# Values of the next key group fetched and split four steps later in a one-core attention block

## The chip, the cores and the metric

The kernel runs on one core of one Trainium2 chip. The metric is the device time of one execution in microseconds (us), taken as the median of several runs. The core has five engines that matter here: TensorE (PE in the profile, with its weight loads shown apart as PEld), VectorE (DVE), ScalarE (ACT), GpSimd (POOL) and SyncE (SP), which issues most of the loads.

## The reference, cut to what matters

The block is one layer of a hybrid generator over 512 latent tokens of width 2048, with 256 context tokens, all in float32. Attention has 12 query heads of width 128 in 4 key groups, three heads to a group. The keys and values of a group are 512 latent and 256 context rows, 768 in all:

```
q = _rope(_rmsnorm(heads(h @ w_q)), cos, sin) * q_scale
k = concat(_rope(_rmsnorm(heads(h @ w_k))), _rmsnorm(heads(hc @ w_k)))
v = concat(heads(h @ w_v), heads(hc @ w_v))
attn = softmax(q @ k.T) @ v
y_a = (attn * silu(z_a)) @ w_pa
y_b = (fourier_mix(u_b) * silu(z_b)) @ w_pb
out = rmsnorm(x + gate * ((g_a * y_a + g_b * y_b) @ w_o))
```

## The kernel before, in words

**Numbers in two halves.** Every float32 product is made of three matmuls on split numbers: `split_from` (L177) has ACT write a rounded high part (L178) and DVE the remainder, the low part (L179); `mm3` (L332) then multiplies high by high, high by low and low by high (L334 to L336). So every weight, key and value that comes from memory is loaded into a raw buffer, split by ACT and DVE, and only then used by PE.

**Stages.** The projections come first (eight groups of weight products, written in `Group.steps`, L1041), and leave queries, keys, values and gates in DRAM (`qz_d`, `k_d`, `v_d`, `g_d`). Attention follows, from about 815 us to 1015 us of the profile: a loop of `NSTEP` = 48 steps (L1639), one for each quarter (128 query rows) of each of the 12 heads, and three steps more that let the last ones end. Then come branch A's projection, the merge and the output projection.

**A step of attention.** Step `i` computes 128 x 768 scores (`scores`, L1475): DVE takes the row maximum (L1486), ACT the exponential (L1488). `turn` (L1500) transposes the exponentials of step `i - 1` on PE (L1504) and splits them (tiles `pth`, `ptl`). `values` (L1511), called at every even step from 4 on, multiplies two steps' worth of them with the group's values: `values(m)` runs at step `2m + 4`, and its matmuls write `banks` and read `pth`, `ptl` (a row `banks<-pth,s`). Its transposes of the gate path have the line L1519. A key group serves 12 score steps, and since `values` comes four steps after the first of its scores, group n's keys are first used at step 12n and its values at step 12n + 4.

**Work between the steps.** `filler` (L1432) computes branch B's projection as 64 small parts spread over the steps, by `fill`. It has four chunks; each needs two pieces of weights (`("pab", j, pc)`), and fetches them with its first part: chunks 1, 2 and 3 at steps 11, 23 and 36. The modulation's gate rows (`use_gate`, L1321, DVE line L1324) are used at the 16 steps of `GATE_STEPS`.

**The list of loads.** `stream` (L196) puts every piece that is to be loaded on one list, `todo`, in the order in which it will be asked for. `start_load` (L199) takes the list's head, gives it a raw buffer of those that are free, and has SP issue the DMA (L214); `load_more` (L225) does that as long as a raw buffer is free and fewer than eight pieces are ahead. In attention there are seven raw buffers: four of the pool `wp`, `raw1`, and two that are given back at step 33. `get` (L293) hands out the piece that is next on the list. It first splits that piece, and those of the next two that are loaded already, but a piece of values (`"V"`) only when it is itself asked for; a piece of keys or a gate row is handed out raw. Taking a piece out frees its raw buffer for the list's head.

**Keys and values.** `stream_keys` (L406) lists the keys of a group and right behind them its values. `get_keys` (L1340), called at steps 10, 22 and 34 for groups 1, 2 and 3, transposes the keys on PE (L1344), splits them into two tiles of `tiles` (L372), and gets the values, which are split into two more. These tiles are slots of a free list (`take`, L322: the slot that has been free for the longest goes first; `give` puts one at the end), which also serves the exponentials, the queries and branch A's operands. `values` gives a group's four slots back after its last use.

**Who sets the order.** The code's order is a priority only. The framework's planner lays down each engine's order of instructions before the run; it lets an instruction go ahead of earlier code when by its own estimate the inputs are there and the tile's slot has been let go. At run time every engine takes its instructions in that order and waits on semaphores.

Of the kernel before, what the change touches and what calls it, by code (L numbers as in the profile page):

```python
# [120 lines left out]
def block_kernel(ctx, tc, xT, ctx_rows, ctx_toks, x, c_row, w_ss, w_gate, vecs, qkg, rope, dft_c, dft_s,  # L121
# [74 lines left out]
    def stream(key, src, *a, **k):  # L196
        todo.append(Piece(key, src if isinstance(src, list) else [src], *a, **k))
# [174 lines left out]
    def tiles(key):  # L372

        new = [take((1024,), F32R) for _ in range(2)]
        kept.setdefault(key, []).extend(new)
        return new
# [28 lines left out]

    def stream_keys(g):  # L406
        stream(("K", g), flat(k_d[g]), NKEY, KT, "raw")
        stream(("V", g), flat(v_d[g]), NKEY, KT, dst=lambda: tiles(g))

    which_ctx = [0]  # L410
# [6 lines left out]
    for g in range(LAST + 1):  # L417
        for name in ONE_GROUP:
            if (g, name) == (LAST, "Q4"):
                stream_keys(0)  # L420
            if g == KV:
                f = CTX_FORMS.index(next(f for n, f, _, _ in PRODUCTS if n == name))
                stream(("cf", name), cf_d[:, :, f].rearrange("i p j c -> p i j c"), 1024, 8, dst=ctx_tiles)
            stream_product(name, g, w_g[g], BY_DVE_GATES)
            for pc in range(4):
                p = context_piece(g, name, pc)
                if p:
                    src, cols = (ctx_toks[p[1]], 1024) if p[0] == "cn" else (ctx_rows[p[1]], 4 * C)
                    stream(p, src, cols, 1, "raw")
                    todo.insert(len(todo) - 4 + pc, todo.pop())  # L430
            for pc in range(4):
                if (g, name, pc) in GATE_AT:
                    q = GATE_AT[g, name, pc]
                    stream(("gate", q), w_gate[q], 1024, 1, "raw")
                    e = todo.pop()
                    at = next(i for i, x in enumerate(todo) if x.key == (name, g, pc))
                    todo.insert(at + 1, e)
# [3 lines left out]
    for n, j in enumerate(CHUNKS):  # L441
        for pc in BRANCH_B:
            stream(("pab", j, pc), w_pab[j, pc], 1024, 2)
        for keys in (False, True):
            while q < 2 * KK and (GATE_STEPS[q - NGATE] < 12 * n + 9 or keys and n + 1 == NKV):
                stream(("gate", q), w_gate[q], 1024, 1, "raw")
                todo[-1].aside = True
                q += 1
            if not keys and n + 1 < NKV:
                stream_keys(n + 1)  # L450
# [877 lines left out]
    qz, qs, kv = {}, {}, {}  # L1328
# [11 lines left out]
    def get_keys(g):  # L1340
        raw = get(("K", g))
        tk = next_wide() if g else flat(pair("y"))
        for t in range(KT):
            nc.tensor.transpose(tk[:, t * P : (t + 1) * P], raw[:, t * P : (t + 1) * P], ident)  # L1344
        keys = tiles(g)
        split_from(tk[:, :NKEY], *(w[:, :NKEY] for w in keys))
        kv[g] = tuple(keys) + get(("V", g))

    def turn_queries(h, tq):
        for t in range(4):  # L1350
            nc.tensor.transpose(tq[:, t * P : (t + 1) * P], qz[h][:, 0, t, :], ident)
        qs[h] = take((2, T), F32R)
        split_from(tq, qs[h][:, 0, :], qs[h][:, 1, :])

    nc.gpsimd.dma_start(turning, rot_d)
    for g, kind in enumerate(KINDS):
        if g == 3:
            jobs += [lambda: None] * 12 + [context_norm, lambda: None, lambda: None, context_spread]
        elif g == KV:
            while jobs:  # L1360
                job()
            assert not any(p[2] == "raw1" for e in ahead for p, _ in e.raws)
        elif g == KV + 1:
            qzs.close()
            gvs, gvp = region("gvp", "right", reuse_waits="tile")
            hl_pools += range(MORE_HL)
        group = Group(g, forms, new_ev, {"qz": qz_done, "kv": kv_done, "gate": gate_done}[kind], {"a": "x", "b": "y", "c": "x"})
        if g == KV:
            group.more = Context()
        for name in ONE_GROUP:  # L1370
            if (g, name) in ((0, "Q4"), (KV + 1, "P1")):
                assert not any(p[2] == "raw0" for e in ahead for p, _ in e.raws)
                load_row(int(g > 0))
            elif (g, name) == (1, "Q5"):
                silu_of_row(0, flat(new_ev()))
            if (g, name) == (0, "P7"):
                raw_pools.remove((rp, 1, "raw0", 1))
            if (g, name) == (0, "Q5"):
                more_hl.append(1)
                look[0] = 4  # L1380
            elif (g, name) == (KV, "P1"):
                nc.scalar.dma_start(turning, rope)
                nc.scalar.dma_start(new_q()[:, 0, 0:2, :], qkg[:, 2:4, :])
            elif (g, name) == (KV, "Q5"):
                with tc.issue_after(last_split[-1][1].ins):
                    scale_tables(turning, new_q()[:, 0, 0:2, :], 1.0)
            elif (g, name) == (KV - 1, "Q3"):
                raw_pools.remove((rp, 1, "raw1", 1))
                hl_pools[:] = [p for p in hl_pools if not isinstance(p, int)]
            elif (g, name) == (KV + 1, "Q6"):  # L1390
                raw_pools += [(rp, 1, "raw1", 1), (gvp, 2, "raw", 2)]
            elif (g, name) == (LAST, "P7"):
                raw_pools.remove((gvp, 2, "raw", 2))
            elif (g, name) == (LAST, "Q3"):

                free += [(fms[i], f"s{i}") for i in (4, 5, 6, 7, 12, 13, 14, 15, 8, 9, 10, 11, 2, 3, 0, 1)]
                for h in range(2):
                    load_head(h)
            elif (g, name) == (LAST, "Q4"):
                hl_pools[:] = [p for p in hl_pools if not isinstance(p, int)]  # L1400
                get_keys(0)
                jobs.append(lambda: turn_queries(0, pair("y")[:, 0, :]))
            group.run(name)
    gvs.close()
# [234 lines left out]
    for i in range(NSTEP + 3):  # L1639
        h, t = divmod(i, 4)  # L1640
        if i < NSTEP:
            if t == 2 and h + 2 < NH:
                load_head(h + 2)
            if i % 12 == 10 and i // 12 + 1 < NKV:
                get_keys(i // 12 + 1)
            scores(i)
        want = min(3 + 61 * (i + 1) // NSTEP, 64) + (i == NSTEP - 1)
        if want > filled:
            fill(1)
            filled += 1  # L1650
        if i % 2 == 0 and i >= 4:
            values((i - 4) // 2)
        if 1 <= i <= NSTEP:
            turn(i - 1)
            divide(i - 1)
        if t == 1 and h + 1 < NH:
            turn_queries(h + 1, b1())
        if want > filled:
            fill(want - filled)
            filled = want  # L1660
        n = next((n for n, at in enumerate(SUM_AT) if at <= i < at + 3), None)
        if n is not None:
            step = i - SUM_AT[n]
            if step == 0:
                weight_sum(n)
            else:
                summed[-1][step]()
            if step == 2:
                give(summed.pop()[0])
        if i == 3:  # L1670
            with tc.issue_after(maxima[0].ins), tc.issue_after(maxima[1].ins):
                e = take((1024,))
                silu_of_row(1, e)
                give(e)
        if i == 33:
            for p in more_raw:
                raw_pools.remove(p)
                retired.append(p)
                if not any(r is p for a in ahead for r, _ in a.raws):
                    free.append(p[0::2])  # L1680
        if i in GATE_STEPS:
            n = NGATE + GATE_STEPS.index(i)
            use_gate(n, get_aside(("gate", n)), maxima[0])
            if n == 2 * KK - 1:
                raw_pools.append((rp, 1, "raw0", 1))
        for q, name in {43: [(0, "Z5"), (0, "S3")], 44: [(0, "S2")], 45: [(0, "S4")], 47: [(1, "Z5")], 48: [(1, "S3")],
                        49: [(1, "S2"), (1, "S4")]}.get(i, ()):
            branch_forms(q, name)
        if i == NSTEP - 1:
            a_groups.append(a_group(0))  # L1690
            first = a_groups[0].steps("P1")
        if NSTEP > i - 2 >= NSTEP - 3:
            next(first)
            next(first)
# [322 lines left out]
```

## Time and profile before

| what | value |
|---|---|
| median of 3 runs | 1298.21 us (1296.13 to 1298.47) |
| the profiled execution's own time | 1296.16 us |
| its span, first to last instruction | 1294.4 us |
| PE busy | 1276.4 us, 99% |
| DVE busy | 994.9 us, 77% |
| ACT busy | 684.6 us, 53% |
| mean granted TensorE clock | 0.996 |

The span is what the profile shows; the profiled execution's own time is 1.76 us longer, and lies near the lower end of the three runs. Lines such as L178 and L179 are those of a helper, so an instruction is told by its tiles: `s<-wr 128x768` is the split of a group's values (keys are split from `banks`, weights into `whi` and `wlo`). In a timeline a row has the start, the length, the engine with its line, the operation, the tiles, the shape, the count, and in brackets the idle time ahead of it with what ended it. An engine with a q, such as SPq, is the engine's queue; for a row that joins several DMA issues the length runs from the first to the end of the last.

### The profile page before, as it was taken

The page shows a single profiled execution, that of the slowest core. Times are in us where ns is not written, and L with a number is a line of the kernel's source. Part 1 is how long each engine was busy: PE and PEld are TensorE (multiplying, and loading weights), DVE is VectorE, ACT ScalarE, POOL GpSimd, SP SyncE. Part 2 cuts the span into 40 slices and gives each one's busy share as a digit, 9 for nine tenths or more (in the row PEclk, how much of TensorE's full clock was granted, in tenths as well). Part 3 has the DMA queues.
Part 4 walks back from the last instruction along what each step waited for, and adds up shares of the span by engine and source line. Part 5 has one row for each costly group of instructions (what it writes and reads, how often), then busy time and mean ns, then how long its engine had stood idle before and what let it go on. Part 6 is the DMA issues. An engine that isn't in the chain of part 4 may idle for free.

```text
span 1294.4 us, 17700 instructions
## 1 busy us (share of the span) xinstructions
PE 1276.4 (99%) x6598; PEld 1050.6 (81%) x6598; DVE 994.9 (77%) x1302; ACT 684.6 (53%) x1076; POOL 169.1 (13%) x222
## 2 busy tenths in 40 slices
PE   8999999999999999999999999999999999999997
PEld 4677988888888888888888888888888888888885
DVE  5667899889689787658687656788898777887776
ACT  5322655545456454444344544666667646464554
POOL 0000011110102111012021010012100221211210
PEclk9999999999999999999999999999999999999998
DMA  9999588888899989977879897578852899998985
GB/s 377 411 368 353 194 224 218 245 221 261 200 317 251 253 279 291 289 197 188 278 205 283 266 226 261 179 240 248 272 180 67 250 248 252 247 207 235 222 202 171
DMA packets 104487, 319.61 MB, mean 247 GB/s; under 512 B 9904, under 2 KB 33072, under 8 KB 100432
## 3 DMA queue, kind: packets, MB, share of 16 engines
q1 hardware_dynamic: 55056, 197.86, 42.2%
q0 software_dynamic: 27024, 98.19, 35.7%
q10 hardware_dynamic: 22320, 22.42, 5.1%
q8 instruction: 52, 0.85, 0.3%
q14 instruction: 35, 0.29, 0.1%
HBM read 283.82 MB, written 34.61 MB: 246 GB/s over the span
## 4 chain that ended last, share of the span: by engine, by line
PE 95%; DMA 2%; DVE 1%; ACT 1%; issue 0%; SPq 0%; ACTq 0%; DVEq 0%
PE banks L334 10%; PE banks L335 10%; PE banks L336 10%; PE x L336 9%; PE x L334 9%; PE x L335 9%; PE y L334 8%; PE y L335 8%; PE y L336 8%; PE banks L1504 2%; PE pd L562 2%; PE pb L334 2%; PE pb L335 1%; PE pb L336 1%; PE pc L334 1%; PE pc L336 1%
## 5 line engine op out<-in xcount | busy, mean ns | idle before, releaser
L178 ACT ACTIVATE whi<-R 128x1024 fp32r<-128x1024 f32 x138 | 145.1, 1058 | 138.4 <-PE banks L336 47.2
L179 DVE TENSOR_TENSOR wlo<-R,whi 128x1024 fp32r<-128x1024 f32 x138 | 167.4, 1220 | 54.0 <-ACT whi L178 53.7
L179 DVE TENSOR_TENSOR wlo<-wr,whi 128x1024 fp32r<-128x1024 f32 (+1 forms) x122 | 147.0, 1212 | 66.0 <-ACT whi L178 65.8
L178 ACT ACTIVATE whi<-wr 128x1024 fp32r<-128x1024 f32 (+1 forms) x122 | 127.5, 1051 | 124.3 <-PE y L336 38.3
L334 PE MATMUL banks<-whi,s 128*128 128x512 f32 x396 | 156.9, 396 | 1.6 <-DVE ev L1081 1.0
L335 PE MATMUL banks<-wlo,s 128*128 128x512 f32 x396 | 155.2, 392 | 0.0
L336 PE MATMUL banks<-whi,s 128*128 128x512 f32 x396 | 155.1, 392 | 0.0
L334 PE MATMUL x<-whi,s 128*128 128x512 f32 x352 | 137.1, 390 | 0.0
L336 PE MATMUL x<-whi,s 128*128 128x512 f32 x352 | 137.0, 389 | 0.0
L335 PE MATMUL x<-wlo,s 128*128 128x512 f32 x352 | 137.0, 389 | 0.0
L334 PE MATMUL y<-whi,s 128*128 128x512 f32 x316 | 123.1, 389 | 0.0
L335 PE MATMUL y<-wlo,s 128*128 128x512 f32 x316 | 123.1, 389 | 0.0
L336 PE MATMUL y<-whi,s 128*128 128x512 f32 x316 | 122.8, 389 | 0.0
L287 POOL DMA_DIRECT2D R<-in_w_g x64 | 56.0, 875 | 414.0 <-DVE wlo L179 242.2
L178 ACT ACTIVATE s<-wr 128x512 fp32r<-128x512 f32 (+2 forms) x93 | 60.3, 677 | 74.2 <-DMA wr<-cf_d 25.7
L179 DVE TENSOR_TENSOR s<-wr,s 128x512 fp32r<-128x512 f32 (+2 forms) x93 | 66.9, 748 | 36.8 <-ACT s L178 36.0
L334 PEld LDWEIGHTS banks<-whi,s 128*128 128x128 f32 x396 | 74.4, 188 | 17.2 <-issue 1.4
L336 PEld LDWEIGHTS banks<-whi,s 128*128 128x128 f32 x396 | 74.4, 188 | 15.5
L335 PEld LDWEIGHTS banks<-wlo,s 128*128 128x128 f32 x396 | 74.5, 188 | 14.0 <-DVE wlo L179 0.3
L335 PEld LDWEIGHTS x<-wlo,s 128*128 128x128 f32 x352 | 66.1, 188 | 13.8 <-DVE wlo L179 0.2
L336 PEld LDWEIGHTS x<-whi,s 128*128 128x128 f32 x352 | 66.1, 188 | 13.7
L334 PEld LDWEIGHTS x<-whi,s 128*128 128x128 f32 x352 | 66.1, 188 | 13.6
(319 smaller groups left out, 2824.3 us busy)
## 6 DMA issues: line engine op xcount, KB each, us to landing
wr<-in_w_g SPq DMA_DIRECT2D x128, 512.0 KB, 5.9
R<-in_w_g POOLq DMA_DIRECT2D x64, 512.0 KB, 7.6
wa<-in_w_ss SPq DMA_DIRECT2D x31, 1024.0 KB, 10.0
R<-in_w_g SPq DMA_DIRECT2D x32, 512.0 KB, 5.9
wr<-in_w_gate SPq DMA_DIRECT2D x32, 512.0 KB, 5.2
wr<-in_w_o SPq DMA_DIRECT2D x24, 512.0 KB, 7.4
R<-in_w_o POOLq DMA_DIRECT2D x24, 512.0 KB, 9.3
wr<-in_w_pab SPq DMA_DIRECT2D x20, 512.0 KB, 5.8
```

The source lines that it names most:

```text
L178: first = nc.scalar.activation(hi, src, ACT.Copy)
L179: return first, nc.vector.tensor_tensor(lo, src, hi.bitcast(F32), op=ALU.subtract)
L287: nc.gpsimd.dma_start(chain[e.pc], e.nxt, accum_op=ALU.add)
L334: nc.tensor.matmul(o, ah, bh, start=start, stop=False, skip_group_check=cont)
L335: nc.tensor.matmul(o, ah, bl, start=False, stop=False, skip_group_check=cont)
L336: nc.tensor.matmul(o, al, bh, start=False, stop=stop, skip_group_check=cont)
L562: nc.tensor.matmul(acc[32 * j : 32 * j + 32], c2[:, n, :], w[:, k, :], start=n < 4, stop=n >= KK - 4)
L1504: nc.tensor.transpose(tp[:, k * P : (k + 1) * P], p[:, k * P : (k + 1) * P], ident)
```

## The change

The values of a group are now listed and fetched apart from its keys. For groups 1 to 3 they are listed right behind the weights of branch B's chunk of the same number (the keys stay behind the chunk before), and they are fetched and split at steps 14, 26 and 38 instead of 10, 22 and 34. Group 0 keeps its order. No operation is added or left out.

```diff
     def stream_keys(g):
         stream(("K", g), flat(k_d[g]), NKEY, KT, "raw")
+
+    def stream_values(g):
         stream(("V", g), flat(v_d[g]), NKEY, KT, dst=lambda: tiles(g))
...
             if (g, name) == (LAST, "Q4"):
                 stream_keys(0)
+                stream_values(0)
...
         for pc in BRANCH_B:
             stream(("pab", j, pc), w_pab[j, pc], 1024, 2)
+        if n:
+            stream_values(n)
...
-        kv[g] = tuple(keys) + get(("V", g))
+        kv[g] = tuple(keys)
+
+    def get_values(g):
+        kv[g] += get(("V", g))
...
                 get_keys(0)
+                get_values(0)
...
             if i % 12 == 10 and i // 12 + 1 < NKV:
                 get_keys(i // 12 + 1)
+            if i % 12 == 2 and i > 12:
+                get_values(i // 12)
             scores(i)
```

## The prediction

> **What bounds the kernel now.** The page comes first: span, busy shares, and the engines of the chain that ended last.
>
> ```profile
> span 1294.4 us, 17700 instructions
> PE 1276.4 (99%) x6598; PEld 1050.6 (81%) x6598; DVE 994.9 (77%) x1302; ACT 684.6 (53%) x1076; POOL 169.1 (13%) x222
> PE 95%; DMA 2%; DVE 1%; ACT 1%; issue 0%; SPq 0%; ACTq 0%; DVEq 0%
> ```
>
> PE works for 1276.4 of 1294.4 us and makes 95% of the chain. An edit that leaves PE's work alone, as this one does, can only win time in which PE waits. So the second view is the table of windows over attention, 20 us a row: length, then busy time (and instructions) of PE, PEld, DVE, ACT, POOL, then the granted clock.
>
> ```profile
> 835.00:855.00 20.00, 19.59 (x143) 17.78 (x142) 16.99 (x27) 14.57 (x28) 2.52 (x4) 1.00 0.62 183
> 855.00:875.00 20.00, 19.97 (x132) 17.27 (x131) 16.09 (x27) 10.94 (x24) 3.03 (x5) 1.00 0.80 261
> 895.00:915.00 20.00, 19.74 (x133) 17.11 (x132) 17.06 (x28) 13.78 (x27) 3.01 (x5) 1.00 0.89 285
> 935.00:955.00 20.00, 20.00 (x137) 17.66 (x136) 18.02 (x28) 13.66 (x28) 1.87 (x4) 1.00 0.54 173
> 955.00:975.00 20.00, 19.64 (x135) 17.39 (x134) 16.96 (x29) 13.88 (x27) 1.42 (x2) 1.00 0.58 173
> sum 240.00, PE 237.96 PEld 206.73 DVE 193.93 ACT 157.39 POOL 36.27; mean PE 19.83 PEld 17.23 DVE 16.16 ACT 13.12 POOL 3.02
> ```
>
> The sum is that of twelve such rows, 795 to 1035 us: PE idles 240.00 - 237.96 = 2.04 us in all of attention. DVE is the second engine, up to 18.02 of 20 us busy (935 to 955). Third, whom PE waits for between 795 and 1015 us:
>
> ```profile
> PE banks L334 <- DVE ev L1081: 1.0, 1, 1.0
> PE banks L1504 <- DVE ptl L179: 0.4, 1, 0.4
> PE banks L334 <- ACT s L1488: 0.4, 1, 0.4
> PE banks L334 <- DVE R L1452: 0.2, 1, 0.2
> ```
>
> The 1.0 us comes from the end of the last projection group, which the change does not touch. What is left for it is 0.4 + 0.4 + 0.2 = 1.0 us.
>
> **Where the values are split now.** The code asks for them at steps 10, 22 and 34. The first and last start of the row maxima set the pace, (1002.0 - 815.3) / 47 = 3.97 us a step, so these steps lie near 855, 903 and 950 us. The timelines of ACT, DVE and SP show when it really happens:
>
> ```profile
> L1486 DVE TENSOR_REDUCE gain<-banks x48: 937/950/959, 815.3 to 1002.0; 128x1 f32<-128x768 f32 x48
> ```
>
> ```profile
> 824.65 0.84 ACT L178 ACTIVATE s<-wr 128x768 fp32r<-128x768 f32 x1
> 827.15 0.96 DVE L179 TENSOR_TENSOR s<-wr,s 128x768 fp32r<-128x768 f32 x1 [0.58 <-PE banks L1504]
> 889.12 0.84 ACT L178 ACTIVATE s<-wr 128x768 fp32r<-128x768 f32 x1
> 891.12 0.94 DVE L179 TENSOR_TENSOR s<-wr,s 128x768 fp32r<-128x768 f32 x1
> 940.95 0.84 ACT L178 ACTIVATE s<-wr 128x768 fp32r<-128x768 f32 x1
> 947.54 0.95 DVE L179 TENSOR_TENSOR s<-wr,s 128x768 fp32r<-128x768 f32 x1
> 792.93 0.33 SPq L214 DMA_DIRECT2D wr<-v_d  x1
> 800.23 8.63 SPq L214 DMA_DIRECT2D wr<-in_w_pab  x2
> 828.18 0.32 SPq L214 DMA_DIRECT2D wr<-v_d  x1
> 892.13 0.33 SPq L214 DMA_DIRECT2D wr<-k_d  x1
> 897.29 0.33 SPq L214 DMA_DIRECT2D wr<-v_d  x1
> ```
>
> The planner has long taken the splits out of the code's steps: group 1's runs 30 us early, the others 14 and 9 us (ACT). The first two already lie outside the crowded stretch in which keys and weights are split; only group 3's low part, at 947.54, lies inside one.
>
> **The change, part by part.** Removed and added: nothing. Three loads (0.33 us of SP each), three high parts (0.84 us of ACT) and three low parts (0.94 to 0.96 us of DVE) move. What PE waits for at the end is `values`, whose first matmuls on a new group are these, at steps 16, 28 and 40:
>
> ```profile
> 875.18 0.28 PE L334 MATMUL banks<-pth,s 128*128 128x256 f32 x1
> 923.54 0.30 PE L334 MATMUL banks<-pth,s 128*128 128x256 f32 x1
> 972.83 0.36 PE L334 MATMUL banks<-pth,s 128*128 128x256 f32 x1
> ```
>
> When can the splits start in the changed kernel? Not before their slots are let go. I walked through the free list by hand: taking two slots at steps 14, 26 and 38 gives each split a slot that is let go at step 10 (after `values(3)`, whose gate copy on ACT is the 855.16 row), at step 22 (`turn(21)`, whose split starts at 905.44) and at step 35 (`turn(34)`, 957.88):
>
> ```profile
> 855.16 0.37 ACT L1529 COPY R<-banks 128x256 f32<-128x256 f32 x1
> 905.44 0.81 ACT L178 ACTIVATE pth<-banks 128x768 fp32r<-128x768 f32 x1
> 957.88 0.81 ACT L178 ACTIVATE pth<-banks 128x768 fp32r<-128x768 f32 x1
> ```
>
> So the splits do become later, by some 16 to 31 us, and each has a stretch of its own: 855.2 to 875.2 (20.0 us), 905.4 to 923.5 (18.1 us), 957.9 to 972.8 (14.9 us), for 0.84 + 0.95 = 1.8 us of work. In the windows DVE has free time there: 20 - 16.09 = 3.9 us in 855 to 875, 2.9 us in 895 to 915, 3.0 us in 955 to 975. I cost all three splits at **nothing**, hidden behind matmuls that run anyway. If that cover went, each would cost up to its own 1.8 us.
>
> The stretch that group 3 leaves: PE waits there once behind an exponential.
>
> ```profile
> 954.08 0.95 DVE L1486 TENSOR_REDUCE gain<-banks 128x1 f32<-128x768 f32 x1
> 955.59 0.89 ACT L1488 ACTIVATE s<-banks,gain 128x768 f32<-128x768 f32 x1
> 956.63 0.39 PE L334 MATMUL banks<-s,s 128*128 128x256 f32 x1 [0.36 <-ACT s L1488]
> ```
>
> This exponential needs the maximum at 954.08, and DVE is nearly without a gap from 947.54 until then. Without the 0.95 us at 947.54 the wait of 0.4 us should go: **-0.4 us**. Next late is then ACT itself, which works without a break in front of that exponential, so I take no more.
>
> Loads: the two pieces of chunk 1 (800.23) go ahead of group 1's values (792.93) on SP. The first of these has its split at 811.62, held until PE is done with a buffer of the last projection group, so an earlier landing gains nothing. The values, issued behind them near 809, still land some 40 us ahead of their slot.
>
> ```profile
> 811.62 1.06 ACT L178 ACTIVATE whi<-wr 128x1024 fp32r<-128x1024 f32 x1 [1.66 <-PE x L336]
> ```
> Walking through the list the same way, groups 2 and 3 get the raw buffer `raw1`, behind the gate row of step 13 and behind group 2's split; four gate rows load one to three steps later, each still at least 5 steps (20 us) ahead of its use. Gate rows take 5.2 us from issue to landing, so this costs nothing. Group 3's keys (892.13), which had waited on SP for group 2's values to be split (892.06), are freed of that, with over 50 us in hand before step 34 either way. If a load were late there, the price would be one landing:
>
> ```profile
> wr<-in_w_gate SPq DMA_DIRECT2D x32, 512.0 KB, 5.2
> ```
>
> **Sum:** 1294.4 - 0.4 = 1294.0 us of span. The profiled execution took 1296.16 us, 1.76 more, and stands 2.05 us under the median of the runs shown. So the forecast is 1295.8 for such an execution and 1298.21 - 0.4 = **1297.8 us** for the median. About 0.2% (2.6 us, 1295.6 to 1300.8) is what a measurement of this kernel can tell from no change, so the forecast is no change. Bounds: below, all 1.0 us of PE's waits goes, 1297.2; above, every split is uncovered, 3 x 1.8 = 5.4 us, 1303.6. I take the lower part, since the rows at 855 to 973 show room on both engines.
>
> **The rivals.**
>
> *The split becomes the last thing `values` waits for (slower).* The place is steps 16, 28 and 40. Code order now puts the splits two steps (8 us) ahead of their use, and the planner may leave them there. ACT and DVE serve the splits behind whatever is queued, and this row shows what one late input does on ACT: 1.20 us idle, and the copy and exponential behind it late.
>
> ```profile
> 903.33 1.06 ACT L178 ACTIVATE whi<-wr 128x1024 fp32r<-128x1024 f32 x1 [1.20 <-DMA wr<-in_w_pab]
> ```
>
> If DVE's lag at the split exceeds those 8 us, PE waits for the whole split, 1.8 us, at each group: 1298.2 + 5.4 = 1303.6. For it: group 3's low part lagged its high part by 947.54 - 940.95 = 6.6 us, the point of decision is not far off. Against: the stretches are 15 to 20 us long. From two of three places on, it passes 0.2%.
>
> A wait could also cost clock. The granted clock is 1.00 in every window above, and 0.87 in the first 10 us, where PE is busy for only 6.57:
>
> ```profile
> 0.00:10.00 10.00, 6.57 (x40) 4.51 (x40) 4.19 (x13) 7.08 (x11) 1.91 (x11) 0.87 0.81 292
> ```
>
> The Trainium skill, "TensorE: Matmul & The Clock Gate", section "Part 1: The HAM clock gate", states that an idle window of about 3.4 us halves PE's clock until it has been busy for as long again. By that rule a single wait of 1.8 us costs no clock, and the late split's time stays as worked out; a wait for a whole landing would cost more than its length, and no row of attention shows one of that size.
>
> *Short waits go too (faster).* A matmul that waits less than the profile counts as idle shows as a longer one. In the scores the first of three is 331 - 286 = 45 ns longer than the second:
>
> ```profile
> L334 PE MATMUL banks<-s,s 128*128 128x256 f32 x47 | 15.5, 331 | 0.4 <-ACT s L1488 0.4
> L335 PE MATMUL banks<-s,s 128*128 128x256 f32 x47 | 13.5, 286 | 0.0
> ```
>
> 47 x 45 ns = 2.1 us. If these and the 1.0 us of waits went, it would be 1298.2 - 3.1 = 1295.1. For it: DVE is relieved in three stretches. Against: such a step in length comes with each change of kind of matmul, whatever the other engines do, and the work only moves to other stretches.
>
> *The change doesn't do what it says.* The planner follows data and slots; if it finds slots sooner than I worked out, it puts the splits where they were: 1298.2.
>
> *Another order by chance (slower).* With new priorities the planner's order of PE, ACT and DVE changes all through attention, and a kernel with 2.04 us of PE idle time has less to win than to lose: twice that idle, plus one landing of 5.2 us, would be 1298.2 + 2 + 5.2 = 1305.4.
>
> **How the numbers follow.** Forecast 0.36, unchanged placement 0.12, late split 0.21, another order 0.14, short waits 0.17. So same 0.36 + 0.12 = 0.48, slower 0.21 + 0.14 = 0.35, faster 0.17. The likeliest is 1297.8. The range reaches from the faster case's 1295.1 to the late split's 1303.6, and leaves out about half of the faster case and half of the other order's, 0.16 in all.
>
> **What would show it.** Right: the rows `s<-wr 128x768` lie between 855 and 875, 905 and 923, 958 and 973; PE's matmuls at 875, 923 and 973 wait for no `L179 s<-wr`; the wait behind L1488 near 956 is gone; PE idles 1 to 2 us between 795 and 1035. Wrong: a PE row `banks<-pth,s` with idle time `<-DVE s L179` near those times, SP holding a gate row until its use, or PE's idle in the windows changed by over 2 us. A change of over 2.6 us with unchanged idle would mean that the matmuls themselves got longer or shorter, and that I looked in the wrong place.

## The result, and the profile after

The changed kernel takes 1300.12 us (median of 22 runs, 1299.14 to 1303.41), the kernel before 1297.93 us in the 22 runs beside them (1296.13 to 1300.28). The ratio is **1.002** (95% interval 1.0015 to 1.0026): 2.2 to 2.6 us slower. The median lies inside the range on record, and still inside the 0.2% that the prediction called no change; but the interval leaves out 1. The kernel did become slower, and that was not the forecast. The profiled execution of the changed kernel took 1300.13 us, its span is 1298.4 us; that is 4.0 us more than the profiled execution before, which lies 1.8 us under the median of its kernel.

In the changed kernel the lines named here have moved by 5 or 9: L1081 is now L1086, L1488 is L1497, L1504 is L1513, L1519 is L1528, L1529 is L1538. The page first: span, busy times, and the shares of the chain that ended last.

```profile
span 1298.4 us, 17716 instructions
PE 1278.0 (98%) x6598; PEld 1051.0 (81%) x6598; DVE 994.7 (77%) x1302; ACT 684.0 (53%) x1076; POOL 168.8 (13%) x222
PE 92%; DVE 3%; DMA 2%; ACT 2%; issue 1%; SPq 0%; DVEq 0%; ACTq 0%
```

The counts of PE, DVE and ACT are those of before, so no work was added; PE's share of the chain fell from 95% to 92%, DVE's and ACT's rose. The order of PE's work outside attention is unchanged too. So attention is to be measured, from the first matmul on `banks` to the last one that reads `pth`. The first two rows are the kernel before, the others the changed one (start, length, engine and line, operation, tiles).

```profile
812.57 0.47 PE L334 MATMUL banks<-whi,s 128*128 128x512 f32 x1 [0.98 <-DVE ev L1081]
1016.61 0.28 PE L336 MATMUL banks<-pth,s 128*128 128x256 f32 x1
```

```profile
813.73 0.47 PE L334 MATMUL banks<-whi,s 128*128 128x512 f32 x1 [0.98 <-DVE ev L1086]
1020.03 0.28 PE L336 MATMUL banks<-pth,s 128*128 128x256 f32 x1
```

1016.61 - 812.57 = 204.04 us before, 1020.03 - 813.73 = **206.30** us after: 2.26 us longer, which is what the medians say (1300.12 - 1297.93 = 2.19). The same windows as in the prediction tell where (length, then busy time and instructions of PE, PEld, DVE, ACT and POOL, the granted clock, the share of the DMA engines, GB/s):

```profile
995.00:1015.00 20.00, 18.46 (x115) 15.64 (x114) 18.92 (x32) 15.73 (x28) 4.59 (x6) 1.00 0.47 84
sum 240.00, PE 236.81 PEld 204.97 DVE 192.26 ACT 155.36 POOL 35.68; mean PE 19.73 PEld 17.08 DVE 16.02 ACT 12.95 POOL 2.97
```

In the three windows to which the splits were to move, PE works within 0.2 us of what it did (19.96, 19.70 and 19.82 us from 855, 895 and 955 on). The one that group 3's low part left, 935 to 955, lost DVE work as foreseen (18.02 to 16.47). PE's idle time in the twelve windows grew from 2.04 to 240.00 - 236.81 = 3.19 us, where the prediction's sign of being right was 1 to 2. The loss is in a row that the prediction does not quote: **995 to 1015 us**, the end of attention, where PE is busy for 18.46 of 20 us and was busy for all 20 before. The list of whom PE waits for between 795 and 1020 us (total, times, longest) says the same:

```profile
PE banks L334 <- DVE ev L1086: 1.0, 1, 1.0
PE banks L334 <- ACT pth L178: 0.9, 1, 0.9
PE banks L334 <- ACT s L1497: 0.5, 1, 0.5
PE banks L334 <- DVE s L179: 0.3, 1, 0.3
PE banks L1513 <- DVE ptl L179: 0.2, 1, 0.2
```

The first is the end of the last projection group, as before. The 0.9 and the 0.5 are new. PE's rows at that place in the changed kernel:

```profile
1003.33 0.39 PE L336 MATMUL banks<-whi,s 128*128 128x512 f32 x1
1003.86 0.44 PE L1513 MATMUL banks<-ident,s 128*128 128x128 f32 x2
1005.20 0.39 PE L334 MATMUL banks<-pth,s 128*128 128x256 f32 x1 [0.90 <-ACT pth L178]
1006.08 0.51 PE L334 MATMUL banks<-whi,s 128*128 128x512 f32 x1 [0.49 <-ACT s L1497]
```

A matmul's shown length reaches into the next one, so starts are the better measure. From 1003.33 to 1006.08 the three steps take 0.53, 1.34 and 0.88 us; the same kinds of matmuls without a wait follow each other after 0.24, 0.13 and 0.22 us in the kernel before (starts at 1004.04, 1004.28 and 1004.41, and at 1005.56 and 1005.78). That is 2.75 - 0.59 = 2.2 us, about all of the loss.

Why PE waits there is seen on ACT. The last exponentials (L1488 before, L1497 after) are, first in the kernel before, then in the changed one:

```profile
1000.16 0.90 ACT L1488 ACTIVATE s<-banks,gain 128x768 f32<-128x768 f32 x1 [0.36 <-DVE s L179]
1002.96 0.90 ACT L1488 ACTIVATE s<-banks,gain 128x768 f32<-128x768 f32 x1
```

```profile
1002.82 0.90 ACT L1497 ACTIVATE s<-banks,gain 128x768 f32<-128x768 f32 x1
1005.05 0.90 ACT L1497 ACTIVATE s<-banks,gain 128x768 f32<-128x768 f32 x1
```

By the tiles' numbers in the order laid down, the two of before are step 47, then step 46: the planner let the last step pass the one before it. In the changed kernel it laid down 46, then 47. Branch A's first product writes into the banks in which the scores of step 47 lie, and its matmuls on weights are the work that could fill PE while it waits for the last transposes and splits. Before, those banks are free from 1000.16 + 0.90 = 1001.1 us on, and nine of these matmuls fill PE from 1002.12 to 1004.28. After, they are free from 1005.95 us on: the matmul at 1006.08 is the first of them, and it waits for just this exponential (`<-ACT s L1497`).

### The profile page after: what moved, and what is told of

Same layout as the page of the kernel before. It is cut to its first block, busy times and chain, and to the rows that moved or that the text cites. A ratio compares the mean times of both kernels' runs of the same rounds, so it can differ in the third digit from the quotient of the medians.

```text
span 1298.4 us, 17716 instructions
## 1 busy us (share of the span) xinstructions
PE 1278.0 (98%) x6598; PEld 1051.0 (81%) x6598; DVE 994.7 (77%) x1302; ACT 684.0 (53%) x1076; POOL 168.8 (13%) x222
## 4 chain that ended last, share of the span: by engine, by line
PE 92%; DVE 3%; DMA 2%; ACT 2%; issue 1%; SPq 0%; DVEq 0%; ACTq 0%
PE banks L334 10%; PE banks L335 10%; PE banks L336 10%; PE x L334 9%; PE x L335 9%; PE x L336 9%; PE y L334 7%; PE y L335 7%; PE y L336 7%; PE banks L1513 2%; PE pd L567 2%; PE pb L334 1%; PE pb L335 1%; PE pb L336 1%; PE pc L334 1%
## 5 line engine op out<-in xcount | busy, mean ns | idle before, releaser
L179 DVE TENSOR_TENSOR wlo<-R,whi 128x1024 fp32r<-128x1024 f32 x138 | 167.6, 1220 | 53.4 <-ACT whi L178 53.1
L179 DVE TENSOR_TENSOR wlo<-wr,whi 128x1024 fp32r<-128x1024 f32 (+1 forms) x122 | 147.0, 1212 | 70.0 <-ACT whi L178 69.9
L179 DVE TENSOR_TENSOR s<-wr,s 128x512 fp32r<-128x512 f32 (+2 forms) x93 | 66.8, 748 | 35.9 <-ACT s L178 35.3
L334 PEld LDWEIGHTS x<-whi,s 128*128 128x128 f32 x352 | 66.1, 188 | 13.6
```

Source lines behind the costliest of these rows:

```text
L179: return first, nc.vector.tensor_tensor(lo, src, hi.bitcast(F32), op=ALU.subtract)
L334: nc.tensor.matmul(o, ah, bh, start=start, stop=False, skip_group_check=cont)
```

## The experiments

All ratios are against the kernel before in runs taken beside them on the same chip, with 95% intervals. "Attention" is the length in us, measured as above in one profiled execution (204.0 before, 206.3 after). The last column gives the last two exponentials in the order laid down. In the first four expectations theory A is the reading above: the order of the last two steps costs the time, the moved splits cost nothing. Its rival says that the later splits cost time in themselves. Theory C, of the second four, widens A to any accident of the planner's order; G, of the last four, is what the second four led to.

| run | what it is | ratio | attention | last exponentials |
|---|---|---|---|---|
| e1 | change, step 47 first | 1.0009 (1.0001 to 1.0018) | 204.8 | 47, 46 |
| e2 | before, step 46 first | 1.0035 (1.0023 to 1.0047) | 208.2 | 46, 47 |
| e3 | change for groups 1, 2 | 1.0054 (1.0041 to 1.0066) | 212.3 | 47, 46 |
| e4 | change for group 3 | 1.0077 (1.0064 to 1.0089) | 205.5 | 47, 46 |
| e5 | e3, one weight split later | 1.0002 (0.9993 to 1.0010) | 203.8 | 47, 46 |
| e6 | e4, store early, 47 first | 1.0009 (1.0000 to 1.0017) | 205.3 | 47, 46 |
| e7 | late splits, old loads | 1.0079 (1.0066 to 1.0091) | 212.5 | 47, 46 |
| e8 | change for group 1 | 1.0027 (1.0017 to 1.0037) | 208.6 | 47, 46 |
| e9 | new loads, old splits | 0.9999 (0.9990 to 1.0008) | 203.5 | 47, 46 |
| e10 | e8, groups 2, 3 loaded later | 1.0008 (0.9999 to 1.0016) | 204.8 | 47, 46 |
| e11 | e3, group 3 loaded later | 1.0025 (1.0016 to 1.0035) | 206.4 | 46, 47 |
| e12 | before, store late | 1.0062 (1.0049 to 1.0075) | 204.1 | 47, 46 |

### The last two steps: e1 and e2

e1 is the changed kernel with step 47's scores laid down ahead of step 46's; e2 is the kernel before with step 47's held behind step 46's maximum and exponential. The main part of e1's edit (`scores` now takes its banks from outside):

```diff
+            if i == NSTEP - 2:
+                w46, w47 = next_wide(), next_wide()
+                scores(i + 1, w47)
+                with tc.issue_after(maxima[0].ins), tc.issue_after(maxima[1].ins):
+                    scores(i, w46)
+            elif i < NSTEP - 1:
-            scores(i)
+                scores(i)
```

> The changed kernel with the last two score steps exchanged: step 47's scores are laid down ahead of step 46's, as the planner has them in the kernel before (there the exponentials end 47, 46; in the changed kernel 46, 47). Theory A (the loss lies at the end of attention: branch A's first product writes the banks that step 47's exponential reads last, so PE waits once the order is 46, 47): the two waits near 1004 and 1005 us go, ratio to before 1.000 (0.9995 to 1.0006). Theory B (the loss is made at the group changes, where the values are split later, and spread over attention): ratio stays at 1.0017 to 1.002.

> The kernel before with one order held: step 47's scores behind step 46's. Values are fetched and split where they were. Theory A: PE waits at the end of attention as in the changed kernel, 1.4 to 2 us, ratio 1.001 to 1.0016. Theory B: no change, ratio 1.000 within 0.0004.

e1 measured 1.0009. Its list of waits between 795 and 1020 us has lost the 0.9, and of the 0.5 there is left:

```profile
PE banks L334 <- ACT s L1497: 0.3, 1, 0.3
```

Attention is 1.5 of the 2.26 us shorter. By this length the order of two exponentials carries about two thirds of the change's loss; by the ratios, 1.0009 against 1.0020, about half, with intervals that overlap. Theory A's band ended at 1.0006, so e1 lies between the theories, nearer to A. e2 lost more than the change and about twice what theory A gave it, 4.1 us, nearly all of it at the end of attention, where both exponentials come at 1006.6 and 1007.5 us and PE stands for 2.1 us:

```profile
1007.63 0.44 PE L1504 MATMUL banks<-ident,s 128*128 128x128 f32 x2 [2.15 <-ACT s L1488]
```

Its hold sets step 46's exponential later than the change does (190.7 us after attention's first matmul, against 189.1), and PE's clock was at half for 3.4 us behind the wait (last section). So e2 shows the direction, not the size.

### A dose of the change: e3 and e4

The change for groups 1 and 2 alone, and for group 3 alone; the other groups keep their loads and splits. e3's edit of the changed kernel (e4 has `(3,)`, e8 below `(1,)`):

```diff
-        if n:
+        if n in (1, 2):
             stream_values(n)
...
                 stream_keys(n + 1)
+                if n + 1 not in (1, 2):
+                    stream_values(n + 1)
...
                 get_keys(i // 12 + 1)
-            if i % 12 == 2 and i > 12:
+                if i // 12 + 1 not in (1, 2):
+                    get_values(i // 12 + 1)
+            if i % 12 == 2 and i // 12 in (1, 2):
                 get_values(i // 12)
```

> The change made for groups 1 and 2 alone; group 3's values as before. The planner then lays down the last exponentials as before, 47, 46. Theory A: ratio 1.000 (0.9996 to 1.0005). Theory B: two thirds of the loss, ratio 1.0013.

> The change made for group 3 alone. The last exponentials are laid down as before, 47, 46. Theory A: ratio 1.000 (0.9996 to 1.0005). Theory B: a third of the loss, ratio 1.0007; a rival C (group 3's late values alone disturb the end of attention, whatever the order): the whole loss, 1.0015 to 1.002.

Both came out far from theory A, and from its rival too: a part of the change costs about three to four times as much as the whole (1.0054 and 1.0077 against 1.002). The doses do not add up, so theory A was incomplete. Each dose has an accident of its own. In e3 ACT stands for 6.6 us, and PE behind it:

```profile
917.49 0.57 SPq L214 DMA_DIRECT2D wr<-in_w_pab  x1
922.53 1.06 ACT L178 ACTIVATE whi<-wr 128x1024 fp32r<-128x1024 f32 x1 [6.60 <-DMA wr<-in_w_pab]
```

```profile
PE banks L334 <- DVE ptl L179: 6.8, 2, 6.6
```

The planner had put the split of a weight piece (`whi<-wr`, the second piece of branch B's chunk 3) ahead of a probability split in ACT's order. SP issued its load only at 917.49, and ACT takes its instructions in order: what PE needed next stood behind it, ready.

In e4 the last exponentials stand as before, and attention is only 1.5 us longer, by three waits of PE of 0.3 to 0.4 us behind `ptl` between 850 and 970; the rest is lost after it, where PE waits for a DRAM add of branch B's result (`s<-yb_d`), twice:

```profile
PE banks L1629 <- DMA s<-yb_d: 7.0, 2, 5.1
```

```profile
1015.11 1.20 POOL L1714 DMA_DIRECT2D gs<-gcol  x1 [0.52 <-issue]
1029.34 0.88 POOL L1615 DMA_DIRECT2D s<-yb_d  x1 [0.59 <-DVE s L1613]
1049.15 1.97 PE L1629 MATMUL banks<-ident,s 128*128 128x128 f32 x8 [5.06 <-DMA s<-yb_d]
```

The transfer issued at 1029.34 served PE at 1049.15, 19.8 us later. On the same queue, 14 us ahead of it, stands the store of the gate's column, `gs`: 128 x 16 single numbers. The kernel before issues it at 996.89 us.

### The accidents taken away: e5 and e6

e5 is e3 with group 3's keys, values and the weight piece that is split ahead of them held behind step 28's exponential; e6 is e4 with `gs` stored right behind the last gate row and step 47 first.

```diff
+            if i == 29:
+                line = maxima[:]
             if i % 12 == 10 and i // 12 + 1 < NKV:
-                get_keys(i // 12 + 1)
+                with ExitStack() as held_behind:
+                    if i // 12 + 1 == 3:
+                        for m in line:
+                            held_behind.enter_context(tc.issue_after(m.ins))
+                    get_keys(i // 12 + 1)
...
```

> The kernel of e3 (the change for groups 1 and 2 only), with group 3's keys, values and the weight piece that is split ahead of them held behind step 28's maximum and exponential, so that the planner lays the weight split down some three probability tiles later. Theory C (the moved splits cost nothing; the loss is whatever order the planner happens to write, here one split of a weight piece in ACT's order ahead of its load): the 6.6 us stall near 920 goes, the last exponentials stand in the order step 47, step 46 as before, and the time comes to the kernel before's, ratio 1.000 +- 0.001, against 1.0054 for e3. Theory D (two doses of the later split cost time themselves, by crowding DVE and ACT before values): the stall moves to another wait of several us, ratio 1.003 to 1.006.

> The kernel of e4 (the change for group 3 only), with the store of the gate's column (gs) issued right behind the last gate row, ahead of the loads of g_d on POOL, and step 47's scores laid down ahead of step 46's. Theory C: e4's loss of 10 us came from the late store of 128x16 single numbers, behind which loads landed late, and from the last two steps' order; both go, ratio 1.000 to 1.001, and PE's wait of 7.0 us behind s<-yb_d goes. Theory E (the late store is a companion, and the branch B tail loses time for another reason, such as the place of the loads of g_d): the wait behind s<-yb_d stays, ratio 1.005 to 1.008.

e5 measured 1.0002: with two of three splits late, no stall and the old end, nothing is lost. e6 measured 1.0009, and its only wait behind `s<-yb_d` is 0.3 us. Theory C's bands held in both. (e6's expectation puts a part of e4's loss on the last two steps; they stood as before in e4 already, so that part of the edit only kept them there.)

### The two halves of the change: e7 and e9

The change does two things: it splits the values later, and it lists their loads behind the next chunk's weights. e7 does only the first. e9 does only the second: the changed list, with each piece of values marked so that it can be taken and split out of the list's order, at steps 10, 22 and 34 as before. e7's edit of the kernel before:

```diff
         stream(("V", g), flat(v_d[g]), NKEY, KT, dst=lambda: tiles(g))
+        if g:
+            todo[-1].aside = True
...
+            if i % 12 == 2 and i > 12:
+                get_values(i // 12)
```

> The kernel before with its list of loads untouched; only the splits of the values of groups 1 to 3 are put four steps behind the keys' (the raw values wait in their buffers until then). The last exponentials stand as before, step 47 ahead of step 46, and the store of the gate's column is early. Theory C: the place of the splits is worth nothing by itself, ratio 1.000 +- 0.001. Theory F (the split close ahead of its use costs time in itself, 1.8 us at each of three groups when uncovered): PE waits behind L179 s<-wr at the first values of a group, ratio 1.002 to 1.004.

> Half of the change: the values of groups 1 to 3 are loaded behind the next chunk's weights, as in the change, but asked for and split with their keys, as before. In the order laid down the last exponentials stand as before (step 47, then 46) and the store of the gate's column is early. Theory G (what costs time is an entry of an in-order queue that is not ready: late splits hold two raw buffers, and a weight piece that is loaded behind the next values then comes late for its place in ACT's order; loads behind the weights can't do that): ratio 1.000 +- 0.001, no wait of PE over 1.1 us in attention. Theory D (the new place of the loads costs something by itself, values late behind weights): PE waits behind L179 s<-wr or ACT idles behind wr<-v_d, ratio 1.002 or more.

e9 came out as expected (0.9999). **e7 missed both theories** by far: 1.0079, although the end stands as before and PE waits for none of the moved splits (its 0.3 us behind `s L179` is at 905.48, ahead of group 2's at 910.19). It has e3's accident twice:

```profile
847.94 0.33 SPq L214 DMA_DIRECT2D wr<-v_d  x1
856.77 0.33 SPq L214 DMA_DIRECT2D wr<-in_w_pab  x1
862.60 1.06 ACT L178 ACTIVATE whi<-wr 128x1024 fp32r<-128x1024 f32 x1 [2.75 <-DMA wr<-in_w_pab]
925.68 1.06 ACT L178 ACTIVATE whi<-wr 128x1024 fp32r<-128x1024 f32 x1 [4.77 <-DMA wr<-in_w_pab]
```

So it is no accident of one order but a mechanism. A late split holds the raw buffer of its values for longer (group 1's: until about 856 us, where before its split was done at 828). The next loads, which SP issues in the list's order, wait for a raw buffer each. In the old list group 2's values (847.94) stand ahead of the next weight piece and take the buffer that comes free first; the weights get the next one, 9 us later. In the order laid down, the weights' split stands ahead of the probability split that PE needs next (it follows at 863.57), so both wait for that load; how the planner came to put it there was not shown. In the changed kernel's rows the loads have changed places, and the split runs without a wait:

```profile
847.27 0.33 SPq L214 DMA_DIRECT2D wr<-in_w_pab  x1
856.10 0.33 SPq L214 DMA_DIRECT2D wr<-in_w_pab  x1
865.02 0.33 SPq L214 DMA_DIRECT2D wr<-v_d  x1
854.39 1.05 ACT L178 ACTIVATE whi<-wr 128x1024 fp32r<-128x1024 f32 x1
```

The second half of the change is what makes the first half cheap. This is theory G of the expectations; e10 and e11 below test it.

### The mechanism put to the test: e8, e10 and e11

By it, a stall must stand wherever a late split is followed by values that are loaded by the old list (and none in e4, whose late group is the last). e8 (group 1 alone, the edit of e3 with `(1,)`) should have one near 862; its expectation was written before e7 was known, and still went by theory C. e10 is e8 with the values of groups 2 and 3 listed behind the weights, but split early; e11 is e3 with group 3's so. e10's edit of e8 (a second argument that is true splits the values at once, out of the list's order):

```diff
-        if n in (1,):
+        if n in (1, 2, 3):
             stream_values(n)
+            todo[-1].aside = n in (2, 3)
...
+                    get_values(i // 12 + 1, i // 12 + 1 in (2, 3))
```

> The change for group 1 only; groups 2 and 3 as before. In the order laid down the last exponentials stand as before (step 47, then 46) and the store of the gate's column is early. Theory C: without either accident the time is the kernel before's, ratio 1.000 +- 0.001. Theory D or F (each moved split costs by itself): a third of the change's loss, ratio 1.0007 or more, with the wait behind the split or DVE near 855 to 875.

> The kernel of e8 (group 1's values split late), with the values of groups 2 and 3 loaded behind the next chunk's weights but split with their keys as before. In SP's order both weight pieces of chunk 2 now stand ahead of group 2's values, which in e8 went first; the last exponentials stand as before. Theory G: ACT's idle time of 3.6 us behind wr<-in_w_pab near 862 and PE's stall of 2.8 us behind it go, and the ratio comes from e8's 1.0027 to 1.000 +- 0.001. Theory D (the late split of group 1 costs by itself): the ratio stays at 1.002 or more.

> The kernel of e3 (groups 1 and 2 as changed), with group 3's values loaded behind chunk 3's weights but split with their keys as before. The last exponentials stand in the changed kernel's order (step 46, then 47), the store of the gate's column behind one g_d load or less. Theory G: the stall of 6.6 us near 920 goes, since the weight piece is loaded ahead of group 3's values, and what stays is the loss at the end of attention of some 1.5 to 2 us: ratio 1.001 to 1.002, against e3's 1.0054. Theory D: 1.004 or more.

e8 missed theory C (1.0027), by just this stall; first e8's rows, then e10's.

```profile
850.47 0.33 SPq L214 DMA_DIRECT2D wr<-v_d  x1
859.29 0.33 SPq L214 DMA_DIRECT2D wr<-in_w_pab  x1
865.99 1.06 ACT L178 ACTIVATE whi<-wr 128x1024 fp32r<-128x1024 f32 x1 [3.61 <-DMA wr<-in_w_pab]
869.22 0.58 PE L334 MATMUL banks<-s,s 128*128 128x256 f32 x1 [2.79 <-DVE ptl L179]
```

```profile
847.80 0.33 SPq L214 DMA_DIRECT2D wr<-in_w_pab  x1
855.07 1.06 ACT L178 ACTIVATE whi<-wr 128x1024 fp32r<-128x1024 f32 x1
```

In e10 group 2's values are issued only at 865.57. With the loads exchanged, the 3.61 and the 2.79 us are gone, and the ratio falls to 1.0008 (0.9999 to 1.0016). e11 is the same for the 6.6 us of e3: gone, 1.0054 to 1.0025. What stays in e11 is the end, since its last exponentials stand as in the changed kernel, and so do its waits:

```profile
PE banks L334 <- ACT pth L178: 0.9, 1, 0.9
PE banks L334 <- ACT s L1508: 0.5, 1, 0.5
```

Its 1.0025 is a little over the expected 1.001 to 1.002, and agrees with the change's own 1.002.

### The store alone: e12

The kernel before, with `gs` issued behind the fourth load of `g_d` that is laid down (at 1019.86 instead of 996.89 us), and the orders of PE, ACT, DVE and SP as they were. The added lines, in `load_ga`; `calls` holds its loads so far, and the old place is emptied:

```diff
+        if len(calls) == 3:
+            nc.vector.tensor_tensor(gcol, gparts[:, :KK], gparts[:, KK:], op=ALU.add)
+            nc.vector.tensor_tensor(gcol, gcol, bada[:, 2 * KK :], op=ALU.add)
+            with tc.issue_after(calls[-1].ins):
+                nc.gpsimd.dma_start(gs.rearrange("k p -> p k"), gcol)
```

> The kernel before with one edit: the store of the gate's column (128x16 single numbers) is issued behind the fourth load of g_d for branch A on POOL, near 1018 us, instead of at 996.9 us. Attention's order stays that of the kernel before. Theory: the loads issued behind it land 12 to 22 us after their issue, PE waits behind s<-yb_d near 1044 to 1049 as in e4, and the time is 5 to 9 us longer: ratio 1.004 to 1.007. If e4's loss had another cause: 1.000 to 1.001, no wait behind s<-yb_d over 1 us.

```profile
1047.51 1.40 PE L1625 MATMUL banks<-ident,s 128*128 128x128 f32 x8 [4.63 <-DMA s<-yb_d]
```

1.0062, with attention as before (204.1 us): the place of one store of 8 KB is worth 7 to 8 us here (7.2 by the medians, 8.0 by the ratio). That is most of e4's 10 us, shown by itself. The whole change doesn't pay it: there `gs` stands where it stood.

No run beats the kernel before by more than its interval, and with PE idle for 2.04 us in attention there is little to be won.

## Why the prediction was wrong

**What bounds the kernel** was right: nothing off PE's path paid or cost until PE waited for it.

**Where the splits go** was right to within a few us. The low parts of the changed kernel lie at the very start of 855.2 to 875.2, and in 905.4 to 923.5 and 957.9 to 972.8. The high parts, on ACT, are at 852.79, 905.19 and 962.51: group 1's came 2.4 us ahead of its stretch, so its slot was free earlier than the walk through the free list had it.

```profile
855.07 0.96 DVE L179 TENSOR_TENSOR s<-wr,s 128x768 fp32r<-128x768 f32 x1 [0.33 <-PE banks L1528]
906.33 0.95 DVE L179 TENSOR_TENSOR s<-wr,s 128x768 fp32r<-128x768 f32 x1
963.38 0.96 DVE L179 TENSOR_TENSOR s<-wr,s 128x768 fp32r<-128x768 f32 x1 [0.34 <-ACT s L178]
```

No matmul of `values` waits for them, so **nothing** was the right price, and the rival of the late split did not happen. (PE's 0.3 us behind `s L179` is at 901.61, 5 us ahead of group 2's split: another tile. The 0.2 us behind `ptl`, at 963.09, end with a low part that DVE began at 962.09, ahead of group 3's.)

**The -0.4 us** near 956 came: the changed kernel's list has no wait behind L1497 there. It is lost in what follows.

**Loads** were costed at nothing with the words that an earlier landing gains nothing. That was right for the sum and missed the point: e7 and e9 show that without this half the late splits cost 1.0079. The prediction named the raw buffers and looked at each load's own landing, not at what the held buffer keeps back.

**The step that failed is the sum**, 1294.4 - 0.4 = 1294.0 us. It carries over PE's other waits unchanged, as if the order of everything else in attention stood still; for a new order it has no term. Between 995 and 1015 us the order did change, and 2.2 us were lost there, some 40 us behind the last moved split. The rival "another order by chance" named that and had 0.14; its time, 1305.4, was too high, since it added a landing of 5.2 us that did not come. That the rest of its sum, 1298.2 + 2 = 1300.2, meets the measured time is luck: the 2 us were the idle time that stood in attention already, not these waits. Of the eight kernels in which only loads or splits of values were moved (the change, e3, e4, e7 to e11), six lost 0.2% or more: by the end of attention in the change and e11, a weight piece that was not there in e3, e7 and e8, a late store in e4. None gained. They are relatives and three of them share one mechanism, so their count measures no chance; but with PE at 99% an order that differs has little to win, and 0.14 looks low.

**What stays open**: e1 leaves 1.0009 (1.0001 to 1.0018), of which 0.7 us lie in attention. Its listed waits (1.0, 0.3, 0.3 and 0.2 us) add up to no more than those of the kernel before, so the 0.7 us lie in pauses that the list does not show, and were not taken apart. e1 restores the order, not the times: its first of the two exponentials comes 189.3 us after attention's first matmul, against 187.6 before and 189.1 in the change. Why the planner exchanged the last two steps was not shown either.

## What to carry to other kernels

Where a planner lays down the order, cost a moved operation twice: at its new place, and by what it holds until then (here a raw buffer, and with it the next loads of an in-order queue). Then look at the places where the order is only just right, such as the last steps of a loop, whose banks the next stage waits for: there an exchange of two steps was worth 1.5 of the 2.3 us lost, while the moved work itself cost nothing. When a part of a change costs more than the whole, look for one entry of an in-order queue that is not ready and holds back what stands behind it.

## What the runs showed of the hardware

**A wait can cost more than its length.** In e3 the 6.6 us of waiting made attention 8.3 us longer. The windows show why (the figure behind POOL's is the granted clock):

```profile
922.21:925.63 3.41, 0.00 (x0) 0.00 (x0) 2.01 (x2) 2.04 (x3) 0.49 (x1) 0.50 0.00 0
925.63:929.04 3.41, 3.27 (x14) 3.18 (x15) 2.23 (x4) 1.34 (x3) 1.10 (x3) 0.50 0.74 258
929.04:932.45 3.41, 3.41 (x19) 2.74 (x19) 2.94 (x7) 1.80 (x4) 0.36 (x1) 1.00 0.90 317
```

PE works again from 925.77 us, but at half clock until 929.04: 3.3 us of work at half speed, 1.6 us lost; 6.6 + 1.6 = 8.2. The prediction weighed the rule of the Trainium skill ("TensorE: Matmul & The Clock Gate", "Part 1: The HAM clock gate") that about 3.4 us of idle time halve the clock until PE has been busy for as long; for this stall and its recovery the trace agrees: the clock fell 3.0 us into the idle time, and came back 3.3 us after PE did. But a much shorter idle time did it too: 1.98 us in e7, ahead of its matmul at 865.84, and 2.15 us in e2 and 2.79 us in e8. 1.99 us in e4, at 1140.04, and all waits of up to 1.5 us, those at the kernel's very start and end aside, left it at 1.00.

What tells 1.98 from 1.99 us is in the traces. The half clock behind these waits lasts 3.41 us, or twice that in e3 and e4. Here is e7, then e4, cut into windows of 3.41 us whose edges are those at which the clock changes in the same trace:

```profile
863.52:866.93 3.41, 1.44 (x12) 1.12 (x11) 2.85 (x4) 1.81 (x5) 0.00 (x0) 1.00 0.85 310
866.93:870.34 3.41, 3.41 (x13) 2.72 (x13) 2.61 (x6) 1.75 (x4) 0.53 (x1) 0.50 0.70 258
```

```profile
1135.20:1138.61 3.41, 2.86 (x13) 2.05 (x11) 3.10 (x4) 1.06 (x1) 1.64 (x3) 1.00 1.01 258
1138.61:1142.02 3.41, 1.98 (x13) 1.80 (x14) 0.71 (x1) 1.01 (x2) 0.52 (x1) 1.00 1.03 271
```

e7's idle time lies in one window, in which PE is busy for 1.44 of 3.41 us (42%), and the next window has half clock. e4's is cut by an edge at 1138.61; the emptier window still has 58%, and the clock stays. The other cases agree: windows with 29% (e2, from 1004.92), 18% (e8, from 865.84) and 31% (e4, from 1043.04) were followed by half clock, the change's emptiest one in attention, with 67% (from 1004.58), was not. In e12 one with 45% (from 1041.34) was not, and at e4's start one with 47% (from 5.38) was; so the limit lies near there, is not sharp, and was not tried. So the sentence in the prediction that a wait of 1.8 us costs no clock stands on thin ground, and the measurement decides against the bare 3.4 us: what these traces show to count is PE's busy share of a window, and a wait of about 2 us costs some 1.7 us more when it falls into one.

**One small store slows the loads behind it.** `gs` writes 128 x 16 single numbers by POOL's queue. The first load of `yb_d` is issued 30 us behind it in the kernel before, and 8.3 us behind it in e12 (at 1028.13); the last figure is the time from issue to landing in us, first before, then in e12:

```profile
s<-yb_d POOLq DMA_DIRECT2D x1, 512.0 KB, 11.5
s<-yb_d POOLq DMA_DIRECT2D x1, 512.0 KB, 19.3
```

In e4, 14 us behind the store, it is 19.8 us. e12's two loads just ahead of the store took 5.6 and 9.0 us, the next two behind it 14.0 and 15.4. In the kernel before, the four transfers behind the store took 13.6 to 15.1 us as well, but there PE waited for none of them.
